# A two-layer diffusion block: kept weights at the turns, a re-ordered first phase, split weight rests on GpSimd, output turned on the chip

## Chip, cores and metric

The kernel runs on one core of one Trainium2 chip. The metric is the device time of one execution in microseconds (us). The core has four compute engines that matter here: TensorE (PE, matrix multiply), VectorE (DVE), ScalarE (ACT) and GpSimd (POOL); SyncE (SP) issues most transfers. Each engine works through its own list of instructions in order and waits for semaphores of the others.

## The reference

Two layers over 1024 channels, for 256 latent tokens (`x`) and 256 context tokens (`xc`). In each layer a half-step gated feed-forward network (FFN1), three token mixers on one normalised input, and a second FFN:

```python
def ffn_half(h_stream, m, gain, w):
    h = modulate(rmsnorm(h_stream, gain), m[0], m[1])
    return h_stream + 0.5 * m[2] * swiglu(h, *w)

def trunk_layer(x, xc, p, cos, sin, ctx_out):
    ...
    x = ffn_half(x, ml[0:3], g[0], p['ffn1'])
    xc = ffn_half(xc, mc[0:3], g[0], p['ffn1'])
    h = modulate(rmsnorm(x, g[1]), ml[3], ml[4])
    hc = modulate(rmsnorm(xc, g[1]), mc[3], mc[4])
    u, gq, gk, gv, nq, nk, nv, gates = split_in(h @ p['w_in'])
    uc, gqc, gkc, gvc, nqc, nkc, nvc, gates_c = split_in(hc @ p['w_in'])
    ...
    x = x + ml[5] * merge_branches(y_ssm, y_gqa, y_na, gates, p)
    ...
    x = ffn_half(x, ml[6:9], g[2], p['ffn2'])
    if ctx_out:
        xc = ffn_half(xc, mc[6:9], g[2], p['ffn2'])
    return x, xc
```

`ctx_out` is false in the second layer, so its second FFN works on the latent tokens alone. The modulation vectors `m` come from `silu(c) @ w_ada[l] + b_ada[l]`. The output is `rmsnorm(x, final_g)`, 256 x 1024.

## The kernel before

The residual stream `X` lies with channels on partitions: 8 blocks `k` of 128 channels, and 512 token columns, of which the first 256 (`HALF`) are context and the rest latent. The normalised input of a stage is kept as two tiles, `Hh` (rounded) and `Hl` (the rest).

**Products in three parts.** Every weight block of 128 x 1024 is fetched by an SP transfer into `raw`; ACT rounds it into `whi`; DVE subtracts, `wlo = raw - whi` (`wload`, L73 to L80). PE then runs three matmuls for each pair of blocks (`mm3`, L82 to L85): `whi` with `Hh`, `whi` with `Hl`, `wlo` with `Hh`. `raw`, `whi` and `wlo` have three buffers each, shared by most of the program. A block so serves 24 matmuls, of 512 columns, or of 256 where one stream alone is multiplied.

**The first phase** (`ffn_start`). The first norm and the first modulation vectors are needed before any FFN matmul. ACT squares `X` (L386), DVE adds, PE sums over channels (`nps`), DVE takes the inverse root (`nt`, ten small operations, L122 to L131), PE spreads it (`nR`, L154). Beside it, PE multiplies the first blocks of `w_ada` (`prow`), ACT copies the result (`rows`, L347), PE turns it (`pmod`, L354) and DVE makes `mod` and `coef` of it (L221, L224). `nh` (L173), `Hh` (ACT, L174) and `Hl` (L175) follow. The first four weight blocks of the FFN (`hidden`) are split in between.

**The turns.** An FFN of both streams ends with eight output blocks `m` (`down`): blocks 0 to 3 with both streams at once, then blocks 4 to 7 with the context columns, then 4 to 7 again with the latent ones. While the latent columns are done, the context stream is normalised for the next stage (`ctx_norm`). The next stage starts in `by_stream`: three weight blocks are multiplied with the context columns (`pbs`), while the latent norm is made, and then the same three with the latent columns. There are three such turns: layer 0 from FFN1 to the mixers, layer 0 from FFN2 to layer 1's FFN1, layer 1 from FFN1 to the mixers. (A fourth use of `by_stream`, from the output projection `pwo` to layer 0's FFN2, has no `down` before it.) In each pass over blocks 4 to 7 every weight is fetched and split anew. While FFNs run, a `hook` slips in other work: modulation products on DVE (L206), and the tables of the S5 mixer.

**The mixers.** `proj` (L771) takes 42 weight blocks per layer through `wload`; the six blocks of the S5 input (three per layer) go through `by_stream`. Attention scores `sc`, their exponentials `pr` (ACT L833, DVE L837, L838), transposes `pt` and products `po` stand between the projections on PE. The last 24 projections of a layer are gates.

**The end** (`fin`). ACT squares the last blocks of `X` and multiplies `X` by the gain (`xg`), PE sums (`nps`), DVE takes the root, PE spreads it (`nR`), DVE multiplies three pieces (`o`), and three transfers write the output with channels on partitions; the host transposes it.

The scheduler sorts each engine's instructions by estimated times. `tc.issue_after(...)` bounds that order from below; `anchor[0]` is the last `wlo` subtraction, `pe_anchor[0]` the last matmul.

Of the kernel before, what the change touches and what calls it, by code (L numbers as in the profile page):

```python
# [27 lines left out]
def body(tc, A):  # L28
# [128 lines left out]
    def norm(l, i, s, per=KC):  # L157

        with tc.issue_after(pe_anchor[0]):
            y = norm_rsqrt(norm_total(norm_sum(s)))  # L160
        yield
        with tc.issue_after(pe_anchor[0]):
            R = norm_spread(y)
        for k in range(KC):
            norm_apply(l, i, s, k, R[:, :HALF])
            if k % per == per - 1:
                yield
# [119 lines left out]

    def by_stream(srcs, lat_norm, hook=lambda us: None):

        units = []  # L290
        for src in srcs:
            w, ps = wload(src, 1024), bank("pbs")
            for k in range(KC):
                mm_k(ps[:, :HALF], w, k, 0, HALF)
            hook(2.6)
            next(lat_norm, None)
            units.append((ps, w))
        for ps, w in units:
            for k in range(KC):
                mm_k(ps[:, HALF:], w, k, HALF, T)  # L300
            hook(2.6)
            yield ps

    def ffn_start(tp):
# [4 lines left out]
        with tc.tile_pool(name="st", bufs=1) as st, tc.tile_pool(name="stp", bufs=1, space=PSUM) as stp:  # L309
# [12 lines left out]

            def hidden(f, *js):
                for j in js:
                    w = wload(A["up"][0, 0, f, j], 1024, st, f"{f}{j}")
                    units.append((stp.tile([128, T], F32, name="pgu", tag=f"pgu{f}{j}"), w))

            units, turn = [], [None]

# [15 lines left out]
            def row_copy(pr):  # L345
                rows = st.tile([128, 2, 2, 128], F32, name="rows", tag="rows", bufs=2)
                S.copy(rows, pr.rearrange("p (k m c) -> p m k c", k=2, m=2))  # L347
                return rows
# [8 lines left out]

            def apply(k):
                for i in range(2):
                    for s in range(2):  # L360
                        norm_apply(0, 0, s, k + i, R[:, stream(s)])
# [22 lines left out]
            for k in range(KC):  # L384
                sq = mid_tile(tp, k % 2).bitcast(F32) if k else acc
                squared = S.activation(sq, X[:, k], AF.Square).ins  # L386
# [34 lines left out]
            for s in range(2):  # L421
                row = wp.tile([128, D], F32, name="row", tag="raw")
                nc.scalar.dma_start(row[:1], A["c2"][s:s + 1])
                with tc.issue_after(squared):
# [4 lines left out]
    def ffn(tp, l, n, streams, hook, mids=None, before=None, then=None):  # L429
        i = 2 * n  # L430
# [19 lines left out]

        def down(half, a, b, ms=range(KC), between=None):
            N = b - a
            for turn, m in enumerate(ms):
                if between and turn:
                    next(between, None)
                ps = bank("pd")
                for q0, q1 in ((0, 6), (6, 11)):
                    wh, wl = wload(A["dn"][l, n, half, m][:, 128 * q0:128 * q1], 128 * (q1 - q0))
                    for f in range(q0, q1):
                        w = slice(128 * (f - q0), 128 * (f - q0) + 128)  # L460
                        mh, ml = mids[11 * half + f]
                        mm3(ps[:, :N], wh[:, w], wl[:, w], mh[:, a:b], ml[:, a:b], f == 0, f == 10)
                evac_x(m, ps, l, i, a, b)
                hook(0.014 * (b - a))

        f0 = 0
        if mids is not None:
            f0 = 2
        else:
            mids = {}  # L470
            if both:
                f0 = 2
                first = by_stream([A["up"][l, n, f, j] for f, j in ((0, 0), (0, 1), (1, 0))], norm(l, i, 1), hook)
                up(0, next(first), next(first))
                up(1, next(first))
            else:
                f0 = 1
                acc = norm_sum(1)
                first = unit(0, 0)
                with tc.issue_after(pe_anchor[0]):  # L480
                    y = norm_rsqrt(norm_total(acc))
                second = unit(0, 1)
                with tc.issue_after(pe_anchor[0]):
                    spread = norm_spread(y)[:, :HALF]
                root.append(tp.tile([128, HALF], F32, name="root", tag="root", bufs=1))
                S.copy(root[0], spread)
                up(0, first, second)
        for half in range(2):
# [266 lines left out]
    def mixer(l):  # L755
# [15 lines left out]
        def proj(j, a, b):  # L771
            wh, wl = wload(A["win"][l, j], 1024)
            ps = bank("pp")
# [395 lines left out]
    for l in range(L):  # L1169
        with ExitStack() as fs:  # L1170
# [10 lines left out]
            load_rows(sb)  # L1181
            ts_ = fs.enter_context(tc.tile_pool(name=f"ts{l}", bufs=1))
            pt_ = fs.enter_context(tc.tile_pool(name=f"pt{l}", bufs=2, space=PSUM))
# [8 lines left out]
            ada = ada_work(ap, jp, sb, [(0, j) for j in range(24, 40)] if l == 0 else [(1, j) for j in range(48, 72)])  # L1192
            hook = Filler([gate, s5_work(), ada], 0.62 if l == 0 else 0.55)
# [7 lines left out]
            ffn(tp, l, 0, (0, 1), hook, mids, lambda: hook.finish(gate), ctx_norm())  # L1201
            hook.finish()
            norms_in(None, None)
        mixer(l)
        with tc.tile_pool(name=f"fb{l}", bufs=1) as tp:
            if l == 0:
                with tc.tile_pool(name="ada9", bufs=1) as ap, tc.tile_pool(name="jp9", bufs=1, space=PSUM) as jp:
# [6 lines left out]
                    def ctx_norm():  # L1214
                        hook.finish()
                        yield
                        yield from norm(1, 0, 0, 2)

                    ffn(tp, 0, 1, (0, 1), hook, None, lambda: hook.finish(gate), ctx_norm())
                norms_in(None, None)  # L1220
            else:
                with tc.tile_pool(name="rp", bufs=1, space=PSUM) as rp:
                    norms_in(rp, "norm")
                    ffn(tp, l, 1, (1,), lambda us: None)
                    norms_in(None, None)

    with tc.tile_pool(name="fin", bufs=1) as tp, tc.tile_pool(name="finp", bufs=1, space=PSUM) as fp:
        xg = tp.tile([128, KC, HALF], F32, name="xg")
        o = tp.tile([128, KC, HALF], F32, name="o")

        def idle(n):
            w = fp.tile([128, 128], F32, name="idle", tag="idle")
            with tc.issue_after(pe_anchor[0]):
                for _ in range(n):
                    pe_anchor[0] = PE.matmul(w, ident, ident, start=True, stop=True).ins  # L1235

        idle(4)
        with tc.issue_after(pe_anchor[0]):
            ps = norm_total_late(1)
        y = norm_rsqrt(ps)  # L1240
        for k in range(KC):
            S.activation(xg[:, k], X[:, k, HALF:], AF.Copy, scale=fg[:, k:k + 1])
        idle(9)
        with tc.issue_after(pe_anchor[0]):
            R = norm_spread(y)[:, :HALF]
        for a, b in ((0, 3), (3, 6), (6, 8)):
            V.tensor_mul(o[:, a:b], xg[:, a:b], R.unsqueeze(1).to_broadcast([128, b - a, HALF]))  # L1247
            nc.sync.dma_start(A["out"][:, a:b], o[:, a:b])
    es.close()
# [90 lines left out]
```

## Time and profile before

| what | value |
|---|---|
| time, three runs | 2163.55 us median (2163.53 to 2164.27) |
| the profiled execution's own time | 2166.13 us |
| its span | 2164.0 us |
| PE busy | 2120.0 us, 98% |
| DVE busy | 1636.3 us, 76% |
| ACT busy | 937.1 us, 43% |
| POOL busy | 0.7 us, 6 instructions |
| weight splits | 480 `whi` on ACT, 951 ns each; 480 `wlo` on DVE, 1085 ns each |

The profiled execution was 2.58 us longer than the median of the runs, and 2.13 us of its time lie outside the span. PE is the busy engine, so a time is lost only where PE stands still or its granted clock is below full. A row of the timeline reads: start, duration, engine, line, operation, output and inputs, count, and in brackets the idle time of the engine before it with what ended it.

### The profile page before, as it was taken

Reading aid. Unit: us, or ns where it says so; the run is one execution under the profiler, and the core shown is the slowest. Engines: PE = TensorE matmul, PEld = TensorE weight load, DVE = VectorE, ACT = ScalarE, POOL = GpSimd, SP = SyncE. Lnnn points to the kernel's source line nnn. Section 1 sums busy time; section 2 is a strip of 40 time slices with the busy share of each in tenths; the row PEclk is TensorE's granted clock in tenths of the full one; section 3 lists DMA queues with packets and bytes.
Section 4 is the critical chain, followed back from the end, with each engine's and each line's share of the span. In section 5 each row is a group of like instructions: output and inputs, shape, how many; then the busy total and the mean of one; then the engine's idle time right before and its main releaser. Section 6 shows DMA issues by size and latency. Waiting matters only on the chain. (4 is left out here: it accounts for less than half of the span.)

```text
span 2164.0 us, 32770 instructions
## 1 busy us (share of the span) xinstructions
PE 2120.0 (98%) x12426; PEld 1808.7 (84%) x12426; DVE 1636.3 (76%) x3202; ACT 937.1 (43%) x1632; POOL 0.7 (0%) x6
## 2 busy tenths in 40 slices
PE   7999999999999999999999999999999999999998
PEld 5888888977777888988888888888889878899998
DVE  4997887777776987897777688877947878776665
ACT  3322333467667323422222343323324767754454
POOL 0000000000000000000000000000000000000000
PEclk8999999999999999999999999999999999999999
DMA  9535544633432664575665445455636454464554
GB/s 319 181 122 175 201 165 135 205 122 114 141 108 76 215 222 149 200 233 163 189 204 175 120 166 184 162 171 183 208 87 203 143 176 146 152 213 147 176 195 127
DMA packets 124485, 366.29 MB, mean 169 GB/s; under 512 B 20644, under 2 KB 26532, under 8 KB 124328
## 3 DMA queue, kind: packets, MB, share of 16 engines
q1 hardware_dynamic: 123456, 363.13, 51.1%
q8 instruction: 98, 1.61, 0.3%
q10 hardware_dynamic: 872, 1.07, 0.1%
q14 instruction: 59, 0.48, 0.1%
HBM read 336.22 MB, written 27.93 MB: 168 GB/s over the span
## 5 line engine op out<-in xcount | busy, mean ns | idle before, releaser
L77 ACT ACTIVATE whi<-raw 128x1024 fp32r<-128x1024 f32 (+2 forms) x480 | 455.9, 951 | 917.2 <-PE pgu L84 287.3
L79 DVE TENSOR_TENSOR wlo<-raw,whi 128x1024 fp32r<-128x1024 f32 (+2 forms) x480 | 519.9, 1085 | 237.5 <-ACT whi L77 206.3
L83 PE MATMUL pgu<-Hh,whi 128*128 128x512 f32 (+1 forms) x1360 | 493.4, 364 | 2.9 <-ACT Hh L174 1.5
L84 PE MATMUL pgu<-Hl,whi 128*128 128x512 f32 (+1 forms) x1360 | 492.6, 362 | 0.0
L85 PE MATMUL pgu<-Hh,wlo 128*128 128x512 f32 (+1 forms) x1360 | 492.1, 362 | 0.4 <-DVE wlo L79 0.4
L83 PEld LDWEIGHTS pgu<-Hh,whi 128*128 128x128 f32 x1360 | 255.8, 188 | 44.1 <-ACT Hh L174 3.0
L85 PEld LDWEIGHTS pgu<-Hh,wlo 128*128 128x128 f32 x1360 | 256.0, 188 | 40.8 <-DVE wlo L79 0.9
L84 PEld LDWEIGHTS pgu<-Hl,whi 128*128 128x128 f32 x1360 | 256.1, 188 | 39.6 <-DVE Hl L175 0.6
L85 PE MATMUL pd<-mid,wlo 128*128 128x256 f32 (+1 forms) x836 | 280.9, 336 | 0.0
L83 PE MATMUL pd<-mid,whi 128*128 128x256 f32 (+1 forms) x836 | 280.6, 336 | 0.0
L84 PE MATMUL pd<-mid,whi 128*128 128x256 f32 (+1 forms) x836 | 280.3, 335 | 0.0
L206 DVE SCALAR_TENSOR_TENSOR ajunk<-araw,sb 128x1024 f32<-128x1024 f32 x208 | 255.4, 1228 | 2.7
L83 PE MATMUL pp<-Hh,whi 128*128 128x512 f32 (+1 forms) x672 | 239.7, 357 | 0.9 <-ACT vf L818 0.5
L85 PE MATMUL pp<-Hh,wlo 128*128 128x512 f32 (+1 forms) x672 | 238.2, 355 | 2.4 <-DVE wlo L79 2.4
L84 PE MATMUL pp<-Hl,whi 128*128 128x512 f32 (+1 forms) x672 | 237.7, 354 | 0.0
L84 PEld LDWEIGHTS pd<-mid,whi 128*128 128x128 f32 x836 | 157.3, 188 | 18.2 <-DVE mid L90 0.4
L85 PEld LDWEIGHTS pd<-mid,wlo 128*128 128x128 f32 x836 | 157.2, 188 | 18.1
L83 PEld LDWEIGHTS pd<-mid,whi 128*128 128x128 f32 x836 | 157.2, 188 | 17.7
L85 PEld LDWEIGHTS pp<-Hh,wlo 128*128 128x128 f32 x672 | 127.2, 189 | 18.6 <-DVE wlo L79 2.8
L83 PEld LDWEIGHTS pp<-Hh,whi 128*128 128x128 f32 x672 | 127.2, 189 | 17.5 <-ACT whi L77 1.4
L84 PEld LDWEIGHTS pp<-Hl,whi 128*128 128x128 f32 x672 | 127.3, 189 | 15.6 <-issue 1.1
L271 DVE TENSOR_TENSOR gact<-gact,pgu 128x512 f32<-128x512 f32 x64 | 43.8, 684 | 54.9 <-PE pgu L85 54.6
(317 smaller groups left out, 2856.5 us busy)
## 6 DMA issues: line engine op xcount, KB each, us to landing
raw<-up SPq DMA_DIRECT2D x176, 512.0 KB, 3.6
araw<-ada SPq DMA_DIRECT2D x104, 512.0 KB, 3.9
raw<-win SPq DMA_DIRECT2D x90, 512.0 KB, 3.8
raw<-dn SPq DMA_DIRECT2D x76, 384.0 KB, 3.1
raw<-dn SPq DMA_DIRECT2D x76, 320.0 KB, 3.0
rw<-ada SPq DMA_DIRECT2D x24, 512.0 KB, 3.9
raw<-wout SPq DMA_DIRECT2D x24, 512.0 KB, 3.3
raw<-wp SPq DMA_DIRECT2D x16, 512.0 KB, 3.7
```

Of the source, the lines that this page charges most:

```text
L77: S.activation(hi[:, :n], raw[:, :n], AF.Copy)
L79: anchor[0] = V.tensor_sub(lo[:, :n], raw[:, :n], hi[:, :n].bitcast(F32)).ins
L83: PE.matmul(out, wh, ah, start=first, stop=False)
L84: PE.matmul(out, wh, al, start=False, stop=False)
L85: pe_anchor[0] = PE.matmul(out, wl, ah, start=False, stop=last).ins
L206: V.scalar_tensor_tensor(junk, raw, 1.0, sb[:, s], op0=ALU.mult, op1=ALU.mult, accum_out=mod[:, l, j, s:s + 1])
L271: V.tensor_mul(g[:, :N], g[:, :N], pu[:, :N])
```

## The change

Four parts of the program are edited; the arithmetic stays the same.

- First phase: the transfers of the first four `up` blocks are written apart from their split (`fetch`, `hidden`); the `pmod` step may only be placed behind the last `nt` operation; the split of the first block only behind that and the first `rows` copy; the split of the second behind the first `wlo`, and of the other two behind that. Two small activations (`row`) go behind the `rows` copy too.
- Turns: the eight weight pieces (`khi`, `klo`, four blocks of two pieces) of the context pass are kept and used again in the latent pass, so the second fetch and split are gone. Their room is that of the S5 tables' work, which is finished and closed ahead of the first kept weight (`room`). The context norm is applied in groups of three, three and two blocks instead of two at a time. At the turn into layer 1's FFN1 (`last_bank` in layer 0's second FFN's `by_stream`), the third accumulator lies in a PSUM bank of its own.
- Mixers: the 84 projections subtract on GpSimd (`rest=nc.gpsimd`), and no longer set `anchor[0]`.
- End: `idle` matmuls, `nR` and three multiplications go; PE transposes `xg` (16 transposes of 128 x 128 into `px`), DVE and ACT each scale two pieces of 512 columns per partition by the root, and four transfers of 256 KB leave from two queues. The host does not transpose any more.

```diff
-    def wload(src, n, pool=None, tag=""):
-        raw = (pool or wp).tile([128, 1024], F32, name="raw", tag="raw" + tag)
+    def wload(src, n, pool=None, tag="", keep=None, rest=V):
+        raw = (pool or wp).tile([128, 1024], F32, name="raw", tag="raw" + ("" if keep else tag))
         nc.sync.dma_start(raw[:, :n], src)
+        if keep:
+            hi, lo = (keep.tile([128, n], F32R, name=w, tag=w + tag) for w in ("khi", "klo"))
+            S.activation(hi, raw[:, :n], AF.Copy)
+            anchor[0] = V.tensor_sub(lo, raw[:, :n], hi.bitcast(F32)).ins
+            return hi, lo
...
-        anchor[0] = V.tensor_sub(lo[:, :n], raw[:, :n], hi[:, :n].bitcast(F32)).ins
+        r = rest.tensor_sub(lo[:, :n], raw[:, :n], hi[:, :n].bitcast(F32)).ins
+        if rest is V:
+            anchor[0] = r
         return hi, lo
...
-            w, ps = wload(src, 1024), bank("pbs")
+            w, ps = wload(src, 1024), (last_bank if last_bank and len(units) == 2 else bank)("pbs")
...
             rows = row_copy(pr)
+            early = copied[0]
             ps = in_turn(norm_total, acc)
             y = norm_rsqrt(ps)
-            in_turn(shift_scale, 0, rows)
-            with tc.issue_after(sums[1]):
-                hidden(0, 0)
-                hidden(0, 1)
+            root = sums[1]
+            with tc.issue_after(root):
+                in_turn(shift_scale, 0, rows)
+            raws = [fetch(0, 0), fetch(0, 1)]
+            with tc.issue_after(root), tc.issue_after(early):
+                hidden(0, 0, raws[0])
             blocks += [ada_rows(2), ada_rows(3)]
-            with tc.issue_after(sums[1]):
-                hidden(1, 0, 1)
+            raws += [fetch(1, 0), fetch(1, 1)]
             blocks += [ada_rows(k) for k in range(4, KC)]
             R = in_turn(norm_spread, y)
-            apply(0)
+            apply(0, 1)
+            with tc.issue_after(anchor[0]):
+                hidden(0, 1, raws[1])
+            apply(1, 1)
+            with tc.issue_after(anchor[0]):
+                for j in range(2):
+                    hidden(1, j, raws[2 + j])
...
-                    wh, wl = wload(A["dn"][l, n, half, m][:, 128 * q0:128 * q1], 128 * (q1 - q0))
+                    wh, wl = kept.get((m, q0)) or wload(A["dn"][l, n, half, m][:, 128 * q0:128 * q1], 128 * (q1 - q0), None, f"{m}{q0}" if keep else "", keep)
+                    if keep:
+                        kept[m, q0] = wh, wl
...
-                down(half, 0, HALF, range(4, KC))
-                down(half, HALF, T, range(4, KC), then)
+                kept = {}
+                down(half, 0, HALF, range(4, KC), None, room(), kept)
+                down(half, HALF, T, range(4, KC), then, None, kept)
...
-            wh, wl = wload(A["win"][l, j], 1024)
+            wh, wl = wload(A["win"][l, j], 1024, rest=nc.gpsimd)
...
+            def room():
+                hook.finish(s5)
+                tables_open.close()
+                return fs.enter_context(tc.tile_pool(name=f"kw{l}", bufs=1))
+
             def ctx_norm():
                 hook.finish(ada)
                 yield
-                yield from norm(l, 1, 0, 2)
+                yield from norm(l, 1, 0, 3)
...
-        idle(4)
+        for k in range(KC - 1):
+            S.activation(xg[:, k], X[:, k, HALF:], AF.Copy, scale=fg[:, k:k + 1])
+            turned(k)
         with tc.issue_after(pe_anchor[0]):
             ps = norm_total_late(1)
         y = norm_rsqrt(ps)
-        for k in range(KC):
-            S.activation(xg[:, k], X[:, k, HALF:], AF.Copy, scale=fg[:, k:k + 1])
-        idle(9)
-        with tc.issue_after(pe_anchor[0]):
-            R = norm_spread(y)[:, :HALF]
-        for a, b in ((0, 3), (3, 6), (6, 8)):
-            V.tensor_mul(o[:, a:b], xg[:, a:b], R.unsqueeze(1).to_broadcast([128, b - a, HALF]))
-            nc.sync.dma_start(A["out"][:, a:b], o[:, a:b])
+        S.activation(xg[:, KC - 1], X[:, KC - 1, HALF:], AF.Copy, scale=fg[:, KC - 1:KC])
+        turned(KC - 1)
+        for j in range(2):
+            V.tensor_scalar(o[:, j, :HALF * 2], px[:, j, :HALF * 2], y[:, j:j + 1], None, op0=ALU.mult)
+            nc.sync.dma_start(A["out"][j, :, :HALF * 2], o[:, j, :HALF * 2])
+            S.activation(o[:, j, HALF * 2:], px[:, j, HALF * 2:], AF.Copy, scale=y[:, j:j + 1])
+            nc.scalar.dma_start(A["out"][j, :, HALF * 2:], o[:, j, HALF * 2:])
```

Where the instructions stand, at three places. First, ACT in the first phase, before, from the last square of `X` (into `mid`) on. The `whi` are splits of `up` blocks, `rows` is the copy that PE's `pmod` needs.

```order
L386 ACTIVATE mid_215<-X_67 128x512
L425 ACTIVATE row_580<-row_580 1x1024
L77 ACTIVATE whi_246<-raw_244 128x1024
L426 DMA sdr_102<-row_580 1x1024
L77 ACTIVATE whi_253<-raw_251 128x1024
L347 COPY rows_218<-prow_168 128x512
L425 ACTIVATE row_584<-row_584 1x1024
```

The same stretch of ACT's list now; `raw_244` is the first `up` block as before, and `raw_246` the second.

```order
L400 ACTIVATE mid_215<-X_67 128x512
L337 ACTIVATE whi_318<-raw_246 128x1024
L361 COPY rows_218<-prow_168 128x512
L337 ACTIVATE whi_248<-raw_244 128x1024
L447 ACTIVATE row_580<-row_580 1x1024
L447 ACTIVATE row_584<-row_584 1x1024
```

Both small activations and the first block's split now stand behind the copy; the second block's split still stands ahead of it.

Second, ACT at the turn from layer 0's FFN1 to the mixers, before. The 640- and 768-wide `whi` are `down` weights of the latent pass, the 1024-wide ones the three blocks of `by_stream`; `Hh` are the context norm's blocks.

```order
L174 ACTIVATE Hh_68<-nh_3654,mod_75 128x256
L174 ACTIVATE Hh_68<-nh_3705,mod_75 128x256
L77 ACTIVATE whi_3740<-raw_3738 128x640
L174 ACTIVATE Hh_68<-nh_3709,mod_75 128x256
L77 ACTIVATE whi_3801<-raw_3799 128x1024
L108 ACTIVATE nsq_3847<-X_67 128x256
L174 ACTIVATE Hh_68<-nh_3760,mod_75 128x256
L174 ACTIVATE Hh_68<-nh_3764,mod_75 128x256
L174 ACTIVATE Hh_68<-nh_3768,mod_75 128x256
L77 ACTIVATE whi_3869<-raw_3867 128x1024
```

Now the last kept weights (`khi`) are followed at once by the three blocks of `by_stream`, ahead of all norm work of the latent pass but one square.

```order
L78 ACTIVATE khi_3476<-raw_3474 128x768
L78 ACTIVATE khi_3500<-raw_3498 128x640
L115 ACTIVATE nsq_3566<-X_67 128x256
L82 ACTIVATE whi_3757<-raw_3755 128x1024
L82 ACTIVATE whi_3825<-raw_3823 128x1024
L82 ACTIVATE whi_3891<-raw_3889 128x1024
L115 ACTIVATE nsq_3569<-X_67 128x256
L115 ACTIVATE nsq_3572<-X_67 128x256
```

So the splits of the next stage moved ahead by the whole latent pass, and on SP the six transfers behind the last kept weight are all of `win`.

Third, ACT's list at its end, before: the last squares and the gain products.

```order
L77 ACTIVATE whi_20847<-raw_20845 128x768
L141 ACTIVATE nsq_20920<-X_67 128x256
L77 ACTIVATE whi_20871<-raw_20869 128x640
L141 ACTIVATE nsq_20923<-X_67 128x256
L1242 ACTIVATE xg_20899<-X_67,fg_74 128x256 x2
L141 ACTIVATE nsq_20926<-X_67 128x256
L1242 ACTIVATE xg_20899<-X_67,fg_74 128x256 x6
```

And now:

```order
L148 ACTIVATE nsq_20805<-X_67 128x256
L82 ACTIVATE whi_20739<-raw_20737 128x640
L148 ACTIVATE nsq_20808<-X_67 128x256
L1273 ACTIVATE xg_20767<-X_67,fg_74 128x256 x7
L148 ACTIVATE nsq_20811<-X_67 128x256
L1278 ACTIVATE xg_20767<-X_67,fg_74 128x256
L1283 ACTIVATE o_20768<-px_20769,nt_20818 128x512
```

The last square (`nsq`), on which the last sum waits, stood behind two gain products and now stands behind seven.

## Rows read from the trace of the kernel before

**Rows 1.** The page: span, and busy time of each engine.

```profile
span 2164.0 us, 32770 instructions
PE 2120.0 (98%) x12426; PEld 1808.7 (84%) x12426; DVE 1636.3 (76%) x3202; ACT 937.1 (43%) x1632; POOL 0.7 (0%) x6
```

**Rows 2.** PE's waits, whole span: waited for, us in total, times, longest.

```profile
PE pbs L83 <- ACT whi L77: 7.9, 7, 2.7
...
PE sc L865 <- ACT pr L833: 4.5, 8, 0.9
PE pp L85 <- DVE wlo L79: 2.4, 2, 2.0
```

**Rows 3.** Windows of the three turns, instructions on `pbs` alone (PEclk: granted clock).

```profile
core 0: us, PE busy (x) PEld busy (x) DVE busy (x) ACT busy (x), PEclk, DMA share, GB/s
419.64:442.27 22.63, 19.78 (x144) 18.97 (x144) 0.00 (x0) 1.05 (x2) 0.92 0.60 222
1263.89:1288.63 24.74, 20.70 (x144) 19.81 (x144) 0.03 (x1) 0.58 (x1) 0.86 0.52 185
1649.53:1671.37 21.84, 19.77 (x144) 18.96 (x144) 0.00 (x0) 1.05 (x2) 0.92 0.62 229
```

**Rows 4.** Timeline of PE in the turns: `nR` of the latent norm; two matmuls, eight apart.

```profile
430.77 0.60 PE L154 MATMUL nR<-ident,nt 128*128 128x128 f32 x4
...
1670.29 0.28 PE L83 MATMUL pbs<-Hh,whi 128*128 128x256 f32 x1
...
1671.25 0.28 PE L85 MATMUL pbs<-Hh,wlo 128*128 128x256 f32 x1
```

**Rows 5.** Timeline of ACT in the second of these turns.

```profile
1265.86 1.06 ACT L77 ACTIVATE whi<-raw 128x1024 fp32r<-128x1024 f32 x1 [2.51 <-DMA raw<-up]
```

**Rows 6.** Timeline of PE at the start of layer 0's second FFN.

```profile
916.45 0.50 PE L83 MATMUL pgu<-Hh,whi 128*128 128x512 f32 x1 [1.15 <-ACT gact L270]
```

**Rows 7.** Timelines of ACT, PE and DVE in the first phase.

```profile
21.26 1.06 ACT L77 ACTIVATE whi<-raw 128x1024 fp32r<-128x1024 f32 x1 [2.89 <-DMA raw<-up]
22.22 0.57 ACT L347 COPY rows<-prow 128x512 f32<-128x512 f32 x1
...
22.84 1.86 PE L354 MATMUL pmod<-pick,rows 128*128 128x2 f32 x8 [4.80 <-ACT rows L347]
25.62 2.08 PE L154 MATMUL nR<-ident,nt 128*128 128x128 f32 x8 [0.92 <-DVE nt L131]
...
25.48 2.36 DVE L79 TENSOR_TENSOR wlo<-raw,whi 128x1024 fp32r<-128x1024 f32 x2
27.76 1.26 DVE L173 SCALAR_TENSOR_TENSOR nh<-X,coef,nR 128x256 f32<-128x256 f32 x3
```

**Rows 8.** POOL's timeline; DVE's `wlo` in layer 0's mixers (duration ns min/median/max); two windows.

```profile
1.01 0.29 POOL masks.py:199 TENSOR_SCALAR_AFFINE_SELECT ident<-ident 128x128 f32<-128x128 f32 x1
...
L79 DVE TENSOR_TENSOR wlo<-raw,whi x74: 550/1224/1228, 441.8 to 879.7; 128x1024 fp32r<-128x1024 f32 x63, 128x384 fp32r<-128x384 f32 x11
...
1774.70:1782.00 7.30, 5.33 (x22) 3.77 (x23) 5.69 (x11) 3.50 (x9) 0.00 (x0) 0.77 0.69 217
712.00:760.00 48.00, 48.00 (x212) 39.52 (x211) 47.81 (x73) 17.58 (x23) 0.00 (x0) 1.00 0.67 221
```

**Rows 9.** Timeline at the end; last, DVE's `gact` on the page.

```profile
2154.14 0.40 ACT L141 ACTIVATE nsq<-X 128x256 f32<-128x256 f32 x1
2154.44 2.49 ACT L1242 ACTIVATE xg<-X,fg 128x256 f32<-128x256 f32 x6
2154.59 0.61 PE L147 MATMUL nps<-ones,nsq 128*128 128x1 f32 x4
2157.01 0.16 DVE L131 TENSOR_TENSOR nt<-nt 128x2 f32<-128x2 f32 x1
2159.02 1.79 SPq L1248 DMA_DIRECT2D out_dram<-o  x3
...
L271 DVE TENSOR_TENSOR gact<-gact,pgu 128x512 f32<-128x512 f32 x64 | 43.8, 684 | 54.9 <-PE pgu L85 54.6
```

More of the change, by code (lines that the diff above doesn't have):

```diff
@@ L165, in norm @@
             norm_apply(l, i, s, k, R[:, :HALF])
-            if k % per == per - 1:
+            if k % per == per - 1 or k == KC - 1:
                 yield
@@ L321, in ada_rows, with fetch, hidden @@
                 return w
[L323 to L326, printed above, removed]
+            def fetch(f, j):
+                raw = st.tile([128, 1024], F32, name="raw", tag=f"raw{f}{j}")
+                nc.sync.dma_start(raw, A["up"][0, 0, f, j])
+                return raw
+            def hidden(f, j, raw):
+                hi, lo = (st.tile([128, 1024], F32R, name=w, tag=f"{w}{f}{j}") for w in ("whi", "wlo"))
+                S.activation(hi, raw, AF.Copy)
+                V.tensor_sub(lo, raw, hi.bitcast(F32))
+                units.append((stp.tile([128, T], F32, name="pgu", tag=f"pgu{f}{j}"), (hi, lo)))
+            copied = [None]
             units, turn = [], [None]
@@ L346, in row_copy @@
                 rows = st.tile([128, 2, 2, 128], F32, name="rows", tag="rows", bufs=2)
-                S.copy(rows, pr.rearrange("p (k m c) -> p m k c", k=2, m=2))
+                copied[0] = S.copy(rows, pr.rearrange("p (k m c) -> p m k c", k=2, m=2)).ins
                 return rows
@@ L356, in shift_scale, with apply @@
                     ada_bias(0, m, k, k + 2, src=pt[:, m])
-            def apply(k):
-                for i in range(2):
+            def apply(k, n=2):
+                for i in range(n):
                     for s in range(2):
@@ L423, in ffn_start @@
                 nc.scalar.dma_start(row[:1], A["c2"][s:s + 1])
-                with tc.issue_after(squared):
+                with tc.issue_after(early):
                     S.activation(row[:1], row[:1], AF.Silu)
@@ L427, in ffn_start, with ffn @@
         return mids
-    def ffn(tp, l, n, streams, hook, mids=None, before=None, then=None):
+    def ffn(tp, l, n, streams, hook, mids=None, before=None, then=None, room=None, last_bank=None):
         i = 2 * n
@@ L449, in up, with down @@
                 gate_up_late(tp, mids[f], pg, pu, root[0])
-        def down(half, a, b, ms=range(KC), between=None):
+        def down(half, a, b, ms=range(KC), between=None, keep=None, kept={}):
             N = b - a
@@ L472, in ffn @@
                 f0 = 2
-                first = by_stream([A["up"][l, n, f, j] for f, j in ((0, 0), (0, 1), (1, 0))], norm(l, i, 1), hook)
+                first = by_stream([A["up"][l, n, f, j] for f, j in ((0, 0), (0, 1), (1, 0))], norm(l, i, 1), hook, last_bank)
                 up(0, next(first), next(first))
@@ L1181, in body @@
             load_rows(sb)
-            ts_ = fs.enter_context(tc.tile_pool(name=f"ts{l}", bufs=1))
+            tables_open = ExitStack()
+            ts_ = tables_open.enter_context(tc.tile_pool(name=f"ts{l}", bufs=1))
             pt_ = fs.enter_context(tc.tile_pool(name=f"pt{l}", bufs=2, space=PSUM))
@@ L1197, in ctx_norm @@
                 yield
-                yield from norm(l, 1, 0, 2)
+                yield from norm(l, 1, 0, 3)
             norms_in(pt_, "po")
-            ffn(tp, l, 0, (0, 1), hook, mids, lambda: hook.finish(gate), ctx_norm())
+            ffn(tp, l, 0, (0, 1), hook, mids, lambda: hook.finish(gate), ctx_norm(), room)
             hook.finish()
@@ L1216, in ctx_norm @@
                         yield
-                        yield from norm(1, 0, 0, 2)
-                    ffn(tp, 0, 1, (0, 1), hook, None, lambda: hook.finish(gate), ctx_norm())
+                        yield from norm(1, 0, 0, 3)
+                    with tc.tile_pool(name="kw9", bufs=1) as kp:
+                        ffn(tp, 0, 1, (0, 1), hook, None, lambda: hook.finish(gate), ctx_norm(), lambda: kp,
+                            lambda name: jp.tile([128, T], F32, name=name, tag="pbs"))
                 norms_in(None, None)
@@ L1228, in body, with turned @@
         xg = tp.tile([128, KC, HALF], F32, name="xg")
-        o = tp.tile([128, KC, HALF], F32, name="o")
-        def idle(n):
-            w = fp.tile([128, 128], F32, name="idle", tag="idle")
+        o = tp.tile([128, 2, D], F32, name="o")
+        px = fp.tile([128, 2, D], F32, name="px")
+        def turned(k):
             with tc.issue_after(pe_anchor[0]):
-                for _ in range(n):
-                    pe_anchor[0] = PE.matmul(w, ident, ident, start=True, stop=True).ins
-        idle(4)
+                for j in range(2):
+                    pe_anchor[0] = PE.transpose(px[:, j, 128 * k:128 * k + 128], xg[:, k, 128 * j:128 * j + 128], ident).ins
+        for k in range(KC - 1):
+            S.activation(xg[:, k], X[:, k, HALF:], AF.Copy, scale=fg[:, k:k + 1])
+            turned(k)
         with tc.issue_after(pe_anchor[0]):
@@ L1240, in body @@
         y = norm_rsqrt(ps)
-        for k in range(KC):
-            S.activation(xg[:, k], X[:, k, HALF:], AF.Copy, scale=fg[:, k:k + 1])
-        idle(9)
-        with tc.issue_after(pe_anchor[0]):
-            R = norm_spread(y)[:, :HALF]
-        for a, b in ((0, 3), (3, 6), (6, 8)):
-            V.tensor_mul(o[:, a:b], xg[:, a:b], R.unsqueeze(1).to_broadcast([128, b - a, HALF]))
-            nc.sync.dma_start(A["out"][:, a:b], o[:, a:b])
+        S.activation(xg[:, KC - 1], X[:, KC - 1, HALF:], AF.Copy, scale=fg[:, KC - 1:KC])
+        turned(KC - 1)
+        for j in range(2):
+            V.tensor_scalar(o[:, j, :HALF * 2], px[:, j, :HALF * 2], y[:, j:j + 1], None, op0=ALU.mult)
+            nc.sync.dma_start(A["out"][j, :, :HALF * 2], o[:, j, :HALF * 2])
+            S.activation(o[:, j, HALF * 2:], px[:, j, HALF * 2:], AF.Copy, scale=y[:, j:j + 1])
+            nc.scalar.dma_start(A["out"][j, :, HALF * 2:], o[:, j, HALF * 2:])
     es.close()
@@ L1333 @@
     aps = {n: nc.dram_tensor(n, a.shape, mybir.dt.from_np(a.dtype), kind="ExternalInput").ap() for n, a in arrays.items()}
-    aps["out"] = nc.dram_tensor("out_0_dram", (128, KC, HALF), F32, kind="ExternalOutput").ap()
+    aps["out"] = nc.dram_tensor("out_0_dram", (2, 128, D), F32, kind="ExternalOutput").ap()
     with tile.TileContext(nc) as tc:
```

9 lines of the change are left out of this document (5 added, 4 removed).

## The prediction

> **What bounds the kernel now.** I read the page first: PE is busy for 2120.0 of 2164.0 us and no other engine for more than 76% [rows 1]. The reader is to see that the whole program is a list of PE's work with about 44 us of gaps, and that an edit pays only by closing a gap, by ending a stretch of half clock, or by shortening what stands before the first and behind the last matmul. The second view is PE's waits: the largest is `pbs` for `whi`, 7.9 us in 7 waits; then the softmax chain (`sc` for `pr`) with 4.5 us, and `pp` for `wlo` with 2.4 us [rows 2]. The third is the windows of the three turns, which show what that wait costs in all: 22.63, 24.74 and 21.84 us for the same 144 matmuls, at granted clocks of 0.92, 0.86 and 0.92 [rows 3]. The clock of a turn falls to its lower level behind the wait, so a wait costs more than its own length. Last come the timelines of the first phase and of the end [rows 7, 9], which no share of busy time shows.
>
> **Turns.** The ideal turn is worked out from rows: eight matmuls of 256 columns start 0.96 us after one another at full clock (1670.29 to 1671.25), 0.12 each, so 144 take 17.3 us; `nR` takes 0.60 us, and the sums before it I put at as much or a little less, together 1.1 [rows 4]. That makes 18.4 us. The excess is 4.2 + 6.3 + 3.4 = 14.0 us [rows 3]. Its cause stands in ACT's timeline: at 1265.86 a `whi` of the next stage starts after 2.51 us of waiting for its transfer [rows 5]. The transfer was late because the latent pass fetched and split eight weight pieces again through the same three buffers. The change removes 24 pieces: 24 transfers, 24 ACT copies and 24 subtractions. PE's matmuls all remain. The list of ACT shows the three next splits directly behind the last `khi`, that is, a latent pass (four blocks of 33 matmuls of 0.12, 15.8 us) before they are needed; SP's list has their transfers there too. What still could wait is `nR`, for a root that DVE makes among other work, and the last two context blocks, which the grouping by three leaves behind the last block instead of four. I take 13.5 us of the 14.0; the bounds are 7 (half given back) and 15. `room` makes the first `khi` wait until the table work and its stores are done. ACT's later copies and the whole kept chain stand behind that. It lies ahead of the context pass, under the last of the four both-stream blocks (33 matmuls of twice 0.12 us, 7.9 us each), and I cost it at nothing; if that cover failed, PE would wait for `khi`, and the turn term would fall towards its lower bound.
>
> **The bank.** In layer 0's second FFN, `pgu` waits 1.15 us for ACT's `gact`, which holds the bank [rows 6]. With one more bank for the third accumulator it need not: 1.1 us, bounds 0 and 1.2.
>
> **First phase.** PE's `pmod` waits 4.80 us for `rows`, and `rows` starts at 22.22, right behind a `whi` whose transfer landed at 21.26 [rows 7]. The edit means to put the copy ahead of the splits. But in ACT's list now, the split of the second `up` block still stands ahead of the copy, and SP's list puts that block's transfer where it was. So the copy will end at 22.8 as before and `pmod` at 24.7. The gain is behind it: `nR` follows at once instead of at 25.62, ends near 24.7 + 2.1 = 26.8, and DVE has by then only two `mod`, one `wlo` (half of the 2.36) and `coef` to do, some 1.7 us. So `nh` starts near 26.85 instead of 27.76: 0.9 us. Bounds: 0, if DVE's single `wlo` is late, and 0.9.
>
> **Mixers.** 84 subtractions leave DVE, 1.22 us each [rows 8], 103 us of its time. DVE is off the path for most of it, so this pays only where PE waits for a `wlo` that DVE's queue holds up: 2.4 us in two waits, the longest 2.0 [rows 2], and behind them a stretch of 7.3 us at a clock of 0.77, which costs 7.3 x 0.23 = 1.7 [rows 8]. Together 4.1. The price of the operation on GpSimd is not in the trace. From below it is DVE's 1.22; from above, GpSimd's select of 128 x 128 takes 0.29 us, and eight times that is 2.3 us [rows 8]. I take 2.3, the row of the same engine. The Trainium skill, "GPSIMD Engine Reference", section "Elementwise — side-by-side cycle accounting", has a tensor_tensor there 1.96 times as long as on VectorE, an estimate of 2.4 us by the row of DVE; the sum would be the same. A block feeds 24 matmuls of 512 columns, 24 x 0.24 = 5.7 us, or 2.9 us with one stream; 2.3 fits both, and a `wlo` that ends 1.1 us later is hidden in most places by the block before it. The buffers also come free 1.1 us later, and SP's transfers with them. I allow 1 us for places where a weight is wanted at once, and 2 us for DVE work held up by GpSimd (below). Net: 4.1 - 3 = 1.1 us faster, bounds 5 faster (nothing lost, and the softmax waits of 4.5 shorter by a fifth) and 10 slower.
>
> **End.** Before, the last square ends at 2154.54, the last sum follows at 2154.59, the root is done at 2157.17, the last transfer is issued by 2160.8 and lands by 2164.0 [rows 9]. ACT's list now has five more gain products ahead of that square, 2.49 / 6 = 0.415 each, so the root is 2.1 us later, at 2159.3. Saved is what came behind it: `nR` and three multiplications, 3.6 us to the last issue; in its place stand two scalings of 512 columns on each of two engines, at most the 0.684 of DVE's `gact` from PSUM [rows 9], 1.4 us, and the issues. The last issue comes near 2161, some 0.3 later, and ACT's queue adds its own issue between: 0.5 us slower, bounds 0.3 faster and 1.2 slower.
>
> **Sum.** -13.5 - 1.1 - 0.9 - 1.1 + 0.5 = -16.1. The profiled execution took 2166.13 us, 2.13 of it around the span, so its like would take 2150.0; it stood 2.58 over the median of the runs, so I forecast 2147.4 us. A difference under 0.2%, 4.3 us, can't be told from no change.
>
> **Rivals.**
> 1. *GpSimd's subtraction holds up DVE* (slower). For: DVE is full where the mixers' PE work is densest (47.81 of 48.00 us, with PE at 48.00) [rows 8], and a DVE that stands still for 2.3 us per weight instead of working 1.22 loses 1.1 net, on 84 weights 90 us; the softmax chain, on which PE already waits, runs through DVE. Against: DVE has a quarter of the span idle, and PE holds a block of work ahead. It decides when 16.1 + 4.3 = 20.4 us reach PE, 0.24 us per subtraction. At 0.3 us each, in place of the 2 us allowed: 2147.4 + 25 - 2 = 2170. At half that point, 0.12 each, 10 us: 2155. The Trainium skill, "SBUF — State Buffer", section "Who interferes with whom", speaks for this rival: a DVE instruction with two SBUF inputs and a GpSimd one that reads SBUF shut each other out for the whole instruction. No row of the kernel before can show it, since GpSimd does nothing there beyond the first 1.3 us.
> 2. *The turn gains half.* The latent norm or the kept chain becomes the wait, as the table work or the last context blocks reach past PE's lead. For: in all three turns DVE still does the same norm work. Against: the `wlo` of the latent pass that stood among it on DVE are gone. 13.5 falls to 7: 2154.
> 3. *The first phase is mended in full.* If the second `up` block lands before the copy is due, `pmod` starts 4.8 us earlier. For: the wait is that long. Against: the list and the landing at 21.26. 2147.4 - 4 = 2143.5.
> 4. *The relieved DVE shortens the softmax waits*, with no price for GpSimd: 5 instead of 1.1: 2143.5.
>
> **How the numbers follow.** The forecast gets 0.52, with its own range 2143 to 2152; rival 2 gets 0.14, rivals 3 and 4 together 0.16, rival 1 at the 2155 level 0.10 and beyond its decisive point 0.08. Range: 2140 to 2157 leaves out the 0.08, and a tenth for sums of two cases. Slower: most of the 0.08, 0.06; same: the rest of it and a little of the 2155 level, 0.05; faster: 0.89.
>
> **What would show it.** In the profile after: `pbs` waiting for `whi` gone from PE's waits in the three turns, and each turn near 18.5 us at a clock near 1.0; `rows` still at 22.2 and `nh` near 26.9; 84 POOL rows of about 2.3 us; DVE busy down by about 103 us for the projections and some 20 for the kept pieces (24 x 1.22 x 704/1024); the root at the end near 2.1 us later relative to the last `pd`. The forecast is wrong if PE's waits for `wlo` on POOL, or for `pr` and `Q`, sum to over 10 us, if `khi` shows as a wait, or if POOL rows are longer than 2.9 us, the time of a one-stream block.

## The result, and the profile after

The changed kernel takes 2201.65 us (median of 4 runs, 2197.66 to 2203.96), the kernel before 2163.54: a ratio of 1.0176, 95% interval 1.0158 to 1.0194. It is 38 us slower. I had forecast 2147.4 us and a range to 2157.0.

The page of the kernel after: span, busy time of each engine, and the group of GpSimd's subtractions (busy us, mean ns).

```profile
span 2199.4 us, 32678 instructions
PE 2126.5 (97%) x12412; PEld 1812.4 (82%) x12412; DVE 1620.0 (74%) x3093; ACT 923.7 (42%) x1610; POOL 217.4 (10%) x90
...
L84 POOL TENSOR_TENSOR wlo<-raw,whi 128x1024 fp32r<-128x1024 f32 x84 | 216.7, 2583 | 1747.6 <-ACT whi L82 1713.1
```

The 84 subtractions are there, at 2.58 us each in the mean. But DVE is busy for only 16 us less, where 103 us of splits for the projections and some 20 for the kept pieces left it: its other rows have become some 107 us longer in all, and there is hardly new work (a row that is held up counts as busy). PE's idle time grew from 44 to 73 us. Its waits, whole span, say where:

```profile
PE pt L866 <- DVE pr L863: 13.2, 11, 3.9
PE sc L890 <- DVE Q L822: 13.2, 6, 5.4
PE sc L890 <- ACT pr L858: 12.8, 8, 3.6
PE pmod L368 <- ACT rows L361: 3.5, 1, 3.5
PE pt L866 <- DVE st L861: 2.9, 4, 1.1
PE pbr L92 <- DVE wlo L84: 2.2, 1, 2.2
...
PE pp L92 <- POOL wlo L84: 0.8, 1, 0.8
...
PE pbs L90 <- ACT whi L82: 0.6, 1, 0.6
```

Two things stand here. `pbs` for `whi` fell from 7.9 to 0.6 us [rows 2], and that rest is in layer 0's other `by_stream`. And a new wait, or rather one wait under several names, is in the attention of the mixers, 42 us in the rows for `pr`, `Q` and `st`. Before, `sc` waited 4.5 us for `pr` [rows 2] and 2.8 us for `Q`:

```profile
PE sc L865 <- DVE Q L797: 2.8, 5, 0.8
```

PE hardly waits for GpSimd itself, 0.8 us. The windows of the turns, all instructions, from first `pbs` to what follows the last:

```profile
core 0: us, PE busy (x) PEld busy (x) DVE busy (x) ACT busy (x) POOL busy (x), PEclk, DMA share, GB/s
416.93:435.10 18.17, 18.17 (x155) 18.17 (x154) 9.45 (x32) 6.95 (x13) 2.88 (x2) 1.00 0.53 203
1283.01:1301.60 18.59, 18.46 (x155) 18.26 (x154) 17.94 (x71) 6.82 (x13) 0.00 (x0) 1.00 0.49 172
1662.23:1680.40 18.17, 18.17 (x155) 18.17 (x154) 9.45 (x32) 6.94 (x13) 2.83 (x2) 1.00 0.54 202
```

They took 22.63, 24.74 and 21.84 us before [rows 3] and take 18.2, 18.6 and 18.2 now, at full clock: 14.3 us gained.

What happens in the mixers is seen in one place. DVE's timeline, then GpSimd's, then PE's, at 1789 us:

```profile
1786.32 2.61 DVE L986 TENSOR_TENSOR zp<-t,t 128x256 f32<-128x256 f32 x1
...
1789.19 0.14 DVE L862 RECIPROCAL st<-st 128x1 f32<-128x1 f32 x1
1789.26 0.40 DVE L955 COPY Dk<-lam_r 128x512 f32<-128x512 f32 x1
1789.58 2.56 DVE L863 TENSOR_SCALAR pr<-pr,st 128x512 f32<-128x512 f32 x1
...
1786.02 2.62 POOL L84 TENSOR_TENSOR wlo<-raw,whi 128x1024 fp32r<-128x1024 f32 x1 [3.85 <-ACT whi L82]
1789.38 2.48 POOL L84 TENSOR_TENSOR wlo<-raw,whi 128x1024 fp32r<-128x1024 f32 x1 [0.73 <-ACT whi L82]
...
1792.19 0.78 PE L866 MATMUL pt<-ident,pr 128*128 128x128 f32 x4 [3.92 <-DVE pr L863]
```

GpSimd starts at 1789.38 and ends at 1791.86. The scaling of `pr`, 0.49 us at most in e1 below, starts 0.20 us later on DVE and ends at 1792.14, 0.28 us after GpSimd. PE waits 3.92 us for it. This wait is made of two blocks: the subtraction before, 1786.02 to 1788.64, had already held `zp<-t,t` on DVE for 2.61 us (0.42 before). The copy of `Dk`, which began 0.12 us ahead of GpSimd, kept its 0.40 us. Grouped by line (minimum, median and maximum ns), DVE's rows on the tiles `t`, `pr` and `st` show who is hit:

```profile
L970 DVE TENSOR_TENSOR t<-t,t x12: 681/691/2777, 453.0 to 1831.6; 128x512 f32<-128x512 f32 x12
L977 DVE TENSOR_TENSOR t<-z,E x12: 681/692/2881, 454.9 to 1836.2; 128x512 f32<-128x512 f32 x12
L965 DVE TENSOR_TENSOR t<-pW,E x6: 690/691/692, 451.6 to 1807.3; 128x512 f32<-128x512 f32 x6
...
L863 DVE TENSOR_SCALAR pr<-pr,st x96: 338/485/2557, 465.9 to 1900.4; 128x512 f32<-128x512 f32 x64, 128x256 f32<-128x256 f32 x32
...
L854 DVE TENSOR_REDUCE st<-sc x96: 397/682/694, 460.5 to 1898.1; 128x1 f32<-128x512 f32 x64, 128x1 f32<-128x256 f32 x32
L862 DVE RECIPROCAL st<-st x96: 145/161/166, 465.6 to 1900.2; 128x1 f32<-128x1 f32 x96
L861 DVE TENSOR_TENSOR st<-st x48: 142/158/1319, 465.2 to 1864.5; 128x1 f32<-128x1 f32 x48
```

Instructions that read two tiles of SBUF are stretched, even one of a single column (`st` + `st`, 0.16 to 1.32 us), and so is the scaling of `pr` from SBUF to SBUF. Those with an operand in PSUM (`pW`, `sc`), and the reciprocal with one SBUF operand, are not. Counted over the whole trace, 50 instructions with two SBUF operands, or scalings of `pr`, began inside a subtraction that outlasted their usual length by 0.15 us or more, and all 50 ended behind it; of 59 others that began so none was stretched. The Trainium skill, "SBUF — State Buffer", section "Who interferes with whom", states that a VectorE instruction with two SBUF inputs contends with a GpSimd one that reads SBUF, that a `tensor_scalar` can enter a mode in which it contends too, and that one with at most one SBUF input doesn't outside such modes; the trace agrees.

It works the other way round too. The median subtraction takes 2.40 us; 13 of the 84 take 2.9 to 3.5 us, and each of them began while VectorE was in an instruction of two SBUF operands. So in the merging stretch:

```profile
775.45 1.22 DVE L213 SCALAR_TENSOR_TENSOR ajunk<-rw,sb 128x1024 f32<-128x1024 f32 x1
...
775.48 3.44 POOL L84 TENSOR_TENSOR wlo<-raw,whi 128x1024 fp32r<-128x1024 f32 x1 [7.45 <-ACT whi L82]
```

### The profile page after: what moved, and what is told of

It reads as the page before. It is cut to its first block, busy times and chain, and to the rows that moved or that the text cites. A ratio compares the mean times of both kernels' runs of the same rounds, so it can differ in the third digit from the quotient of the medians.

```text
span 2199.4 us, 32678 instructions
## 1 busy us (share of the span) xinstructions
PE 2126.5 (97%) x12412; PEld 1812.4 (82%) x12412; DVE 1620.0 (74%) x3093; ACT 923.7 (42%) x1610; POOL 217.4 (10%) x90
## 5 line engine op out<-in xcount | busy, mean ns | idle before, releaser
L82 ACT ACTIVATE whi<-raw 128x1024 fp32r<-128x1024 f32 (+3 forms) x428 | 414.3, 969 | 839.6 <-PE pgu L91 279.7
L84 DVE TENSOR_TENSOR wlo<-raw,whi 128x1024 fp32r<-128x1024 f32 (+2 forms) x344 | 378.4, 1103 | 175.6 <-ACT whi L82 151.1
L84 POOL TENSOR_TENSOR wlo<-raw,whi 128x1024 fp32r<-128x1024 f32 x84 | 216.7, 2583 | 1747.6 <-ACT whi L82 1713.1
L91 PE MATMUL pd<-mid,whi 128*128 128x512 f32 (+1 forms) x572 | 206.1, 360 | 0.0
L90 PE MATMUL pd<-mid,whi 128*128 128x512 f32 (+1 forms) x572 | 206.0, 361 | 0.0
L92 PE MATMUL pd<-mid,wlo 128*128 128x512 f32 (+1 forms) x572 | 205.9, 360 | 0.0
L91 PEld LDWEIGHTS pd<-mid,whi 128*128 128x128 f32 x572 | 107.5, 188 | 18.0 <-DVE mid L97 0.4
L92 PEld LDWEIGHTS pd<-mid,wlo 128*128 128x128 f32 x572 | 107.5, 188 | 17.9
L90 PEld LDWEIGHTS pd<-mid,whi 128*128 128x128 f32 x572 | 107.4, 188 | 17.6
```

Of the source, the lines that this page charges most:

```text
L84: r = rest.tensor_sub(lo[:, :n], raw[:, :n], hi[:, :n].bitcast(F32)).ins
L90: PE.matmul(out, wh, ah, start=first, stop=False)
L91: PE.matmul(out, wh, al, start=False, stop=False)
L92: pe_anchor[0] = PE.matmul(out, wl, ah, start=False, stop=last).ins
```

## The experiments

All ratios are to the kernel before, run on the same chip beside it.

**e1: the mixers' subtractions back on VectorE.**

```diff
-            wh, wl = wload(A["win"][l, j], 1024, rest=nc.gpsimd)
+            wh, wl = wload(A["win"][l, j], 1024)
```

> The changed kernel with the mixers' 84 subtractions back on VectorE; all else as changed. Theory L (a GpSimd subtraction shuts out VectorE instructions that read two SBUF operands, or copy-like ones from SBUF to SBUF, for its whole length, and the softmax chain hands that on to TensorE): the two mixers lose what they lost against the kernel before, 26.7 us (first pbs end to first pwo, layer 0) plus 24.0 us (layer 1), so 2201.6 - 50.7 = about 2151 us, and the waits of sc and pt fall back to about 10 us. Rival T (the kept weights, the other order of norm work or the earlier table work disturb the mixers, and the place of the subtraction has little part in it): stays above 2185 us.

Measured: 2150.71 us, ratio 0.9944 (0.9929 to 0.9959). PE's waits for `pr` and `Q` are 4.5 and 2.6 us again. One argument costs 51 us; the rest of the change gains. The page of e1, and DVE's scaling of `pr`:

```profile
span 2146.0 us, 32620 instructions
PE 2109.9 (98%) x12412; PEld 1799.3 (84%) x12412; DVE 1617.7 (75%) x3177; ACT 921.0 (43%) x1610; POOL 0.7 (0%) x6
...
L863 DVE TENSOR_SCALAR pr<-pr,st x96: 340/478/489, 463.4 to 1850.4; 128x512 f32<-128x512 f32 x64, 128x256 f32<-128x256 f32 x32
```

Between the two profiled spans lie 53.4 us: PE is idle for 36.8 us more in the changed kernel, and busy for 16.6 us more with the same 12412 matmuls, at a mean granted clock of 0.987 against 0.996. So the waits cost more than their own length.

**e2: the kernel before with that argument alone.** `wload` got the parameter `rest`, and `proj` passes `nc.gpsimd`.

> The kernel before with nothing but the 84 subtractions moved to GpSimd. Theory L: it loses the same 50.7 us, 2163.5 + 51 = about 2214 us, with t<-z,E on VectorE above 2 us instead of 0.69. Rival T: within 10 us of the kernel before. Rival M (the loss needs both, since the earlier turns bring weights and softmax work to another phase): between, 2175 to 2200 us.

Measured: 2213.36 us, ratio 1.0231 (1.0215 to 1.0246): 51.5 us more. Its three largest waits are those of the changed kernel to the digit (13.2, 13.2, 12.8). So the price doesn't depend on the turns, and rivals T and M fall.

**e3: GpSimd writes, but reads nothing.**

```diff
-        r = rest.tensor_sub(lo[:, :n], raw[:, :n], hi[:, :n].bitcast(F32)).ins
+            for _ in range(2):
+                r = rest.memset(lo[:, :n].bitcast(F32), 0.0)
```

> The changed kernel, but GpSimd fills wlo of the 84 projections with zeros, twice each, instead of subtracting: the rest of these weights is left out of the products, the rows and bytes that GpSimd writes stay, and it reads no SBUF. Theory L: no VectorE row is stretched, the softmax waits fall back to about 10 us, 2147 to 2152 us. Rival W (what hurts is that GpSimd writes SBUF at the same time, or that a wlo and so its buffers come late, or the order of instructions that the scheduler made around GpSimd's work): above 2185 us.

Measured: 2145.72 us, ratio 0.9922 (0.9906 to 0.9939). The same lines of DVE and GpSimd in this kernel:

```profile
L974 DVE TENSOR_TENSOR t<-t,t x12: 678/693/693, 453.3 to 1787.8; 128x512 f32<-128x512 f32 x12
L981 DVE TENSOR_TENSOR t<-z,E x12: 678/691/693, 455.3 to 1790.7; 128x512 f32<-128x512 f32 x12
...
L867 DVE TENSOR_SCALAR pr<-pr,st x96: 341/482/1325, 464.5 to 1848.1; 128x512 f32<-128x512 f32 x64, 128x256 f32<-128x256 f32 x32
...
L88 POOL MEMSET wlo<- x168: 951/955/1238, 431.7 to 1909.0; 128x1024 f32 x168
```

With GpSimd at work for about 2 us per weight still, no instruction of two SBUF operands is stretched. Only the scaling of `pr` still is, to 1.33 us at most, and twice the copy of `Dk`, to 0.83 us. So it is GpSimd's reading that shuts out the two-operand instructions, and its writing too that shuts out the scaling; the second costs PE 2.0 us in waits of `pt` for `pr`. The order of instructions is not the cause: in the two traces it is the same on PE and ACT, and on VectorE it differs in four places. A late `wlo` this run can't exclude, since a `memset` need not wait for `whi` and so comes early; but PE waits only 0.8 us for one in the changed kernel, and e4 gets time back without an earlier `wlo`. With that rival W falls.

**e4: each subtraction in two halves.**

```diff
+        for c in ([slice(0, n)] if rest is V else [slice(0, n // 2), slice(n // 2, n)]):
+            r = rest.tensor_sub(lo[:, c], raw[:, c], hi[:, c].bitcast(F32)).ins
```

> The changed kernel with each GpSimd subtraction cut into two of 512 columns. Theory L: one that is waiting on VectorE gets in between two pieces, a block lasts at most 1.3 us instead of 2.5, and about half of the 51 us comes back: 2170 to 2185 us. Theory L with a lock that GpSimd keeps from piece to piece: as the changed kernel, 2201 us. Rival W: 2201 us or a little more.

Measured: 2179.08 us, ratio 1.0076 (1.0061 to 1.0091). Of the 51 us 22.6 came back. A half takes 1.30 us at the median, and `t<-t,t` takes 1.67 us at most instead of 2.78. The block lasts as long as the instruction, and VectorE gets in between two: a `t<-t,t` that began at 489.86, inside a first half of 489.44 to 490.73, ended at 491.27, and the second half, begun at 490.69, took 1.74 us. The halves still cost 28 us over e1.

**e8: only the gates on GpSimd.** `rest=nc.gpsimd if j >= CH_GATE else V` in `proj`.

> The changed kernel with only the gates (24 of 42 projections per layer) on GpSimd, the others on VectorE. Theory L: beside the gates VectorE merges branches and splits weights, both of two SBUF operands, and few softmax chains run there; between first pbr and first pwo the changed kernel lost 2.5 and 2.1 us, so e1 plus about 5 us, 2152 to 2162 us. Rival (GpSimd costs only where a softmax chain waits, and else relieves VectorE): 2147 to 2151 us.

Measured: 2174.87 us, ratio 1.0056 (1.0042 to 1.0070): 24 us over e1, where I had written about 5. The rows show why: many gates are multiplied ahead, while the attention still runs. Of GpSimd's 48 subtractions 21 stand ahead of 700 us or between 1671 and 1850 us, beside the attention, and PE's waits for `pr` and `Q` are 10.3, 7.9 and 5.3 us. Both theories fail in size; the waits are those of the changed kernel.

**e10: the scaling of `pr` on ScalarE, GpSimd subtracting.**

```diff
-            V.tensor_scalar(p[:, :n], p[:, :n], st[:, 3:4], None, op0=ALU.mult)
+            S.activation(p[:, :n], p[:, :n], AF.Copy, scale=st[:, 3:4])
```

> The changed kernel, GpSimd subtracting, with the scaling of pr (SBUF to SBUF) on ScalarE instead of VectorE. Theory L: this instruction can no longer be shut out, the 13.2 us that pt waits for it go and come back in part as waits for other VectorE work, 2185 to 2194 us. Rival C (the softmax chain is long because VectorE is late with everything, and which engine scales does not matter): 2198 us or more.

Measured: 2202.37 us, ratio 1.0183 (1.0169 to 1.0197), as the changed kernel. PE's waits:

```profile
PE sc L890 <- ACT pr L858: 18.8, 11, 4.4
PE sc L890 <- DVE Q L822: 12.8, 6, 5.4
PE pt L866 <- ACT pr L863: 9.5, 10, 2.4
```

Taking the commonest victim off VectorE frees nothing; rival C was right on this. The likely reason is that VectorE works in order, so that another instruction of two SBUF operands ahead of the chain holds it instead (`t<-t,t`, `z<-Dk,t` and `Q<-rot,Q` all reach over 2 us here). No run separates that from ScalarE's added work, 923.7 to 972.4 us, and from the other order of instructions.

**e9: the turns' edits alone, on the kernel before.** Kept weights, `room`, groups of three and `last_bank`, as in the change.

> The kernel before with the turns' edits alone: kept weights, room, groups of three, last_bank. In the trace of e1 the three turns take 18.3, 18.7 and 18.3 us instead of 22.6, 24.7 and 21.8. If the turns carry what e1 gains and its end gives 1.5 us back: 14.5 us faster than the kernel before, ratio 0.9933. If the first phase carries 3 us of it: 11 to 12 us, ratio 0.9948.

Measured: 2148.92 us, ratio 0.9936 (0.9923 to 0.9950), 13.8 us faster, against 11.2 for e1. So the turns carry the gain of the change, and nothing clear of noise is left for its other parts; 0.9948 lies just inside the interval. Which of the turns' edits pays was not tried.

**e5: the `rows` copy ahead of the second block's split, on e1.**

```diff
-            with tc.issue_after(anchor[0]):
+            with tc.issue_after(early):
                 hidden(0, 1, raws[1])
```

> As e1 (subtractions on VectorE), and the split of the second up block may only be placed behind the rows copy, so that ACT's list has the copy first. Theory F (the copy behind that split costs the 3.3 us that pmod waits in e1): rows starts near 16.5 us, pmod near 19, nh near 23.2 instead of 26, and the time falls by about 3 us against e1, to 2147.7 us. Rival G (the first 60 us are bounded by the transfers, whose engines are busy for 0.92 and 0.78 of them): pmod is early but the gain is gone by 60 us into the span, less than 1 us against e1.

Measured: 2149.82 us, ratio 0.9942 (0.9929 to 0.9954); against e1 nothing. PE's timeline, and one row of ACT's:

```profile
18.29 1.84 PE L368 MATMUL pmod<-pick,rows 128*128 128x2 f32 x8
20.47 2.08 PE L161 MATMUL nR<-ident,nt 128*128 128x128 f32 x8 [0.33 <-DVE nt L138]
24.29 0.79 PE L90 MATMUL pgu<-Hh,whi 128*128 128x512 f32 x1 [1.75 <-ACT Hh L181]
...
28.71 0.79 PE L90 MATMUL pgu<-Hh,whi 128*128 128x512 f32 x1 [1.29 <-ACT Hh L181]
...
27.20 1.06 ACT L337 ACTIVATE whi<-raw 128x1024 fp32r<-128x1024 f32 x1 [2.57 <-DMA raw<-up]
```

The step does what it says: `pmod` at 18.3 (21.2 in e1), first `pgu` at 24.3 instead of 26.5. Then PE waits again at 28.71 for `Hh`, which stands in ACT's list behind the third block's split, and that waits 2.57 us for its transfer. At the first turn, the profiled execution of e5 is 1.6 us behind that of e1. Theory F falls, and G holds in its outcome; its cause is shown in part, by that transfer. PE's granted clock in the first 50 us is 0.83, against 0.90 in e1, but the changed kernel, with e1's list in this phase, has 0.83 too, so the lower clock isn't shown to be this edit's doing.

**e6: another end, on e1.** `norm_total_late` is called ahead of the products `xg`, and `o` and `px` are four tiles each.

```diff
-        o = tp.tile([128, 2, D], F32, name="o")
-        px = fp.tile([128, 2, D], F32, name="px")
+        o = [tp.tile([128, 512], F32, name=f"o{i}") for i in range(4)]
+        px = [fp.tile([128, 512], F32, name=f"px{i}") for i in range(4)]
```

> As e1, with another end: the norm's last square ahead of six gain products in ACT's list, and a tile of its own for each of the four scaled pieces and their sources. Theory S (in the changed kernel the two engines scale in turn because they share a tile, about 1.5 us, and the root is 1.7 us late behind five gain products): from the last pd to the end of the span 9.7 us instead of 12.2, 2148 us. Rival (the last transfer bounds the end): 11.5 to 12.2 us.

Measured: 2147.53 us, ratio 0.9930 (0.9917 to 0.9944). First DVE and ACT of the changed kernel behind the last root:

```profile
2193.11 0.75 DVE L1281 TENSOR_SCALAR o<-px,nt 128x512 f32<-128x512 f32 x1
2194.62 0.75 DVE L1281 TENSOR_SCALAR o<-px,nt 128x512 f32<-128x512 f32 x1 [0.76 <-ACT o L1283]
...
2193.90 0.69 ACT L1283 ACTIVATE o<-px,nt 128x512 f32<-128x512 f32 x1 [3.43 <-DVE o L1281]
...
2195.41 0.69 ACT L1283 ACTIVATE o<-px,nt 128x512 f32<-128x512 f32 x1 [0.82 <-DVE o L1281]
```

The four scalings run one after another, 2193.11 to 2196.10, each waiting for the one on the other engine. In e6 they run side by side:

```profile
2139.16 1.41 DVE L1277 TENSOR_SCALAR o<-px,nt 128x512 f32<-128x512 f32 x2
...
2139.15 1.26 ACT L1279 ACTIVATE o<-px,nt 128x512 f32<-128x512 f32 x2 [0.33 <-DVE nt L138]
```

From the evacuation of the last `pd` (2135.21) to the end of the span (2144.9) it is 9.7 us, as theory S had it, against 12.5 in the changed kernel (2186.85 to 2199.4). The end confirms S (the root is done 3.8 us after that evacuation, not 6.2); the intervals of the times of e1 and e6 overlap.

**e7: both e5 and e6.**

> As e1, with both edits of e5 and e6. Theories F and S: 2145 us, a ratio to the kernel before of about 0.992. By rivals G and that of the end: 2149 to 2151 us.

Measured: 2149.87 us, ratio 0.9939 (0.9926 to 0.9951); no better than e6, and the same as e5. Its end takes 9.7 us too (2139.83 to 2149.5), so the gain of e6's end is not shown in the time. The best kernel that computes all of the reference is e6, some 0.7% faster than the kernel before, though e9 and e1 are not told apart from it.

## Why the prediction was wrong

**Mixers: the step that failed.** The prediction put "2 us for DVE work held up by GpSimd" into a sum whose net was 1.1 us faster. Measured is 50.9 us slower (the changed kernel against e1) or 51.5 (e2). The 4.1 us for waits for `wlo` didn't come either: the 2.4 us of `pp` fell to 0.8, but `pbr` now waits 2.2 us for a `wlo` on VectorE. GpSimd's 2.58 us lie near the 2.3 taken, by luck, since that was scaled from another operation. What failed is the price of the meeting: I treated it as a small share of each subtraction, when it is a block for the rest of GpSimd's instruction, on whatever two-operand instruction VectorE has at its head. The average is 51 / 84 = 0.61 us per subtraction on PE, 2.5 times the point (0.24) from which rival 1 decides. That rival had the mechanism and named the softmax chain, and I gave it 0.08 beyond its decisive point and bounded the term at 10 us. Two signs that I had named came true: the waits for `pr` and `Q` sum to 39 us, and 13 GpSimd rows are longer than 2.9 us. "DVE has a quarter of the span idle" was the wrong argument against it: the softmax chain is a chain, and it is late by the whole block wherever one falls into it. The merging stretch that I named, with DVE at 47.81 of 48.00 us [rows 8], was not the place: between first `pbr` and first `pwo` of the mixers the loss is a few us, and there it is often GpSimd that is held up.

**Turns: right.** 13.5 us forecast, 14.3 by the windows, 13.8 with the bank in e9. The cover of `room` held; no `khi` appears among PE's waits. The bank's 1.15 us [rows 6] is gone from the list of waits, but e9 doesn't time it apart.

**First phase: the direction.** The list read right: `rows` still started behind the second block's split, and `nh` at 26.22 instead of 27.76, against 26.85 forecast. But the first `pgu` differs by 1 to 2 us between executions with one and the same list (26.46 in e1, 27.70 here, 28.39 in e3), so the 1.5 us can't be put down to the edit. What stands ahead of the prediction says that the second block's split is bound by the first `wlo`. It isn't: `hidden` doesn't set `anchor[0]`, and in this phase `norm_apply` sets it last, to an `Hl` on VectorE. In the trace the second `wlo` stands behind such an `Hl` (28.19 after 27.40), and ACT's split does not (20.81). By e5, rival 3 would have paid nothing.

**End: mis-sized.** The forecast was 0.5 us slower. From the last evacuation to the end of the span 12.5 us against 10.7 before: 1.9 slower. The late root was right (2193.01 is 6.2 us after 2186.85; before 3.9). The scalings I had side by side; they ran in turn, 3.0 us instead of 1.4.

## What to carry to other kernels

Before work is moved to GpSimd, list the VectorE instructions that will run beside it and count their SBUF operands: work with a PSUM operand got by here, two SBUF operands and the scaling from SBUF to SBUF didn't, and the price is set by the chain behind the blocked instruction, not by VectorE's idle share. If it must be GpSimd, cut its instructions short (halves took back 22.6 of 51 us here), or let it only write. And when a rule makes a rival, work out the bounds of the term that it acts on by that rule too.

## What the runs showed that I had not expected

An addition of one column was held for over a microsecond (0.16 to 1.32 us). Two engines that scaled separate quarters of one tile ran in strict turn, each waiting for the other, and side by side with a tile each (3.0 against 1.4 us); the waits are the program's, and no run shows a limit of the chip in it. And a first phase that starts its matmuls 2.2 us earlier (e5 against e1) gained nothing in the end.
